# Filler products on TensorE ahead of the norms' sums and other waits, in a two-block transformer kernel

## The chip, the cores and the metric

The kernel runs on one core of a Trainium2 chip. The metric is the device time of one execution in microseconds (us); lower is better. The engines of the core work side by side, each on its own queue of instructions: TensorE (PE in the profile) multiplies matrices, VectorE (DVE) and ScalarE (ACT) work on elements, GpSimd (POOL) too, and SyncE (SP) issues transfers. A queue is worked off in the order in which its instructions stand.

## The reference, cut to what matters

Two blocks, each of two layers, on 512 tokens `x` of 1024 features. The first block has a second stream of 256 context tokens beside `x`; its mixer joins a Fourier transform, an mLSTM recurrence with gates, and a latent attention. The second block has grouped attention and dilated attention. Every layer ends in an MLP with a squared ReLU. What matters here are the norms: each is a sum over the features of every token, and its result scales everything that follows.

```python
def rmsnorm(x, g):
    y = x * rsqrt(mean(x * x, axis=-1) + EPS)
    return y * g
def modulate(h, shift, scale):
    return h * (1 + scale) + shift
...
h  = modulate(rmsnorm(x, g_norm1[l]), sh1, sc1)         # x: 512 tokens
hc = modulate(rmsnorm(xc, g_norm1[l]), sh1c, sc1c)      # context: 256 tokens
pf, mq, mk, mv, mo, mg, cq, ckv, kr = split_proj(h @ w_in[l])
kv = rmsnorm(ckv, g_kvn) @ w_ukv                        # latent keys and values
q  = rmsnorm(cq, g_qn) @ w_uq                           # latent queries
m_t = maximum(inter, dmat.max(axis=-1))                 # mLSTM: running maximum of the gates
...
x = x + ga1 * (concat([y_f, y_m, y_a]) @ w_out[l])
x = x + ga2 * (square(relu(modulate(rmsnorm(x, g_norm2[l]), sh2, sc2) @ w_up[l])) @ w_down[l])
...
return rmsnorm(x, g_final)                              # end of the first block
```

## The kernel before, in words

Features lie on the partitions, so that `x` is eight tiles of [128, 512] and the context eight of [128, 256]. Each product in full accuracy is made of three: an operand is split in a high and a low part, and `mm3` (L136) issues high·high (L143), high·low (L144) and low·high (L146, or L150 after all the others where the product has 256 columns). Weights are streamed in units: a transfer (L127), a cast of the high part on ScalarE (L120), the subtraction for the low part on GpSimd (L121). Two units have a place at a time.

A norm over the features (`norm_r`, L327) sums the squares of the eight blocks on VectorE into `acc` (L325), and lets TensorE multiply the result by a matrix of ones (L333), which adds the 128 partitions up. This sum is a product in plain float32. ScalarE and VectorE make the reciprocal root of it, and then `mod_block` scales, shifts and splits the eight blocks into `h` (L373, L374), which the next products read. The small norms of the latent keys and queries (`rms_small`, L535) do the same with one or two blocks (square L543, sum L548).

`gate_rows` (L856) prepares the gates of the mLSTM: two small products spread the gates over 64 rows (L872, L873), VectorE scans them for a running maximum `m` and a running sum (L883, L884) and subtracts (L888) into `iR`; TensorE then transposes `iR` in six pieces (L891) and spreads `m` over 128 partitions with `emsel`, once per direction (L902).

MLPs and projections whose input is a norm begin with a head (`head`, L401): the first three units of weights are run over the first half of the tokens and then over the second half (`skewed`, L389), so that the second half of the norm has time to be made. The two loops of `mlp` (L447) then run over the other units.

The framework's scheduler places every instruction on its engine's queue from the order in which the builder makes them, with its own estimates; generators in the builder weave independent work between the steps. PSUM, where TensorE writes its sums, is given out by tags (`pm`, `pt`, `p2`), with two places each.

In `build` (L1343) the start of the program runs the first modulation's products round by round (`next(first)`), then the context stream with the norm of `x` ahead, then the two layers of the first block, and then the second block.

Of the kernel before, what the change touches and what calls it, by code (L numbers as in the profile page):

```python
# [26 lines left out]
class Cols:  # L27
    """Per-feature vectors, side by side as columns of one array."""
# [33 lines left out]
def cut(t, H, classes):  # L62
    """The tokens H of t, whose order may be that of the classes modulo 4."""
    return by_classes(t)[:, :, H.start // 4:H.stop // 4] if classes else t[:, H]


def weave(a, b, na, nb):
    """Steps of two generators, in turn: nb of b spread over na of a."""
    credit = 0.0
    for _ in a:  # L70
        credit += nb / na
        while credit >= 1:
            credit -= 1
            if next(b, None) is None:
                credit = -1e9
        yield True
    for _ in b:
        yield True


class Stream:
    """Tokens whose features lie on the partitions: x, eight blocks of [128, n]."""
# [6 lines left out]
class Kernel:  # L89
# [20 lines left out]
    def psum(self, tag, shape):  # L110
        return self.ps.tile(shape, F32, tag=tag, name=tag, bufs=2)

# [10 lines left out]
    def weights(self, src, nk, nm=128, dve=False, extra=None):  # L123
        """A unit of the weights, in two parts; extra: the tag of a third place."""
# [11 lines left out]
    def mm3(self, out, w, xs, ks=None, wide=False):  # L136
        """out += w[:, i].T @ xs[i], each operand in two parts."""
# [3 lines left out]
        for i, (xh, xl) in enumerate(xs):  # L141
            k = ks[i] if ks else i
# [4 lines left out]
        if not wide:  # L147
            # short products leave the low part of the weights more time
# [3 lines left out]
    def rsqrt(self, out, mean_ps, scale, tmp, eps=EPS):  # L152
        """out = (scale * mean + eps) ** -0.5; the tables' result takes a Newton step to float32's accuracy."""
# [9 lines left out]
    def sigmoid(self, out, x, t=None):  # L163
        """out = 1 / (1 + exp(-x)), with no exponential of a positive number; with t, x is read at once."""
# [49 lines left out]
    def mod_cols(self, mod, ps, bias, at, nb, nv):  # L214
        """Rows 32 q + v of the sums to columns: mod[:, v, at + nb q + b]."""
# [3 lines left out]
        pt = self.psum("pt", [128, nb, 128])  # L219
        for b in range(nb):  # L220
# [7 lines left out]
    def gemv_now(self, r, src, out, tag, start, stop):  # L228
        """Round r of the first modulation, for both vectors, in steps, with TensorE's four column groups."""
# [17 lines left out]
    def gemvs_now(self, mod, rounds, src, bias):  # L247
        """Up to four rounds, in one tile of sums."""
# [7 lines left out]
    def gemv_later(self, mod, r, src, bias, vs):  # L256
        """A round of a modulation, in steps, on VectorE."""
# [31 lines left out]
    def until(self, n):  # L289
        """The first n of the modulations' later rounds are done."""  # L290
# [9 lines left out]
    def norm_tag(self, s, H):  # L300
        """Where the tiles of a norm lie: by halves, some are held for long, and have a place of their own."""
# [4 lines left out]
    def norm_add(self, s, k, w=None, H=None):  # L306
        """Takes block k of s.x into the sum of squares, weighted with a column of w; H: of some tokens."""
# [19 lines left out]
    def norm_r(self, s, weighted=False, H=None):  # L327
# [3 lines left out]
        ps = self.psum("pt", [128, n])  # L331
        sums = s.wsums if weighted else s.sums
# [8 lines left out]
    def scaled(self, out, x, a, r, classes):  # L341
        """out = a r x; classes: the tokens of out lie in classes modulo 4."""
# [14 lines left out]
    def norm_mod(self, s, a, sh, r=None, classes=False):  # L357
        """The normed and modulated blocks of s.x, each in two parts."""
        r = self.norm_r(s) if r is None else r
# [19 lines left out]
    def norm_steps(self, s, a, sh, weighted=False, classes=False):  # L379
        """norm_mod by halves of the tokens; the first half's norm_r is done."""  # L380
# [8 lines left out]
    def skewed(self, ws, xs, classes=False):  # L389
        """Some units over the first half of the tokens, then over the second."""  # L390
        for j, H in enumerate(HALVES):
            part = [(cut(h, H, classes), cut(l, H, classes)) for h, l in xs]
            for i, w in enumerate(ws):
# [3 lines left out]
                ps = two[:, t % 2, 0:256] if t in (2, 3) else self.psum("pt" if t == 5 else "pm", [128, 256])  # L397
                self.mm3(ps, w, part, wide=WIDE)
                yield i, H, ps

    def head(self, src, xs, extra, classes=False):  # L401
        """The first units of the products that begin in a norm."""
        return self.skewed([self.weights(src[i], 8, extra=None if i else extra) for i in range(SKEWED)], xs, classes)

    def tail(self, s, src, xs, ga, norm, hook, extra):
        """The last units of the products that end in s.x; hook: when the first half is complete."""
# [20 lines left out]
    def flush(self):  # L427
        """What waits for another unit of products: TensorE's short steps after other engines' work."""
# [7 lines left out]
    def residual(self, s, m, ps, ga, H=slice(None), classes=False):  # L436
        nc, x = self.nc, s.x[m][:, H]
        if classes:
            # from here on the tokens lie in classes modulo 4
# [7 lines left out]
    def mlp(self, ss, up, down, gas, norm=None, aside=None, head=False, hook=None, classes=False):  # L447
        """The streams' MLPs, with each unit of the weights loaded once but for the last units of two streams.
        head: the first two units by halves; hook: the last two as well; classes: s.x takes the order of s.h."""
        norm = norm or self.norm_add  # L450
        lead = 0 if len(ss) == 1 else LEAD
        for c in range(4):
            hid = [[] for _ in ss]
            for i in range(8):
# [7 lines left out]
                if c == 0 and i < lead:  # L462
                    # the first stream's first units: the second's may come later
# [38 lines left out]
    def relu2(self, s, ps, out):  # L502
        """The square of the positive part, in two parts."""
# [11 lines left out]
    # ==== first block ====  # L515
# [19 lines left out]
    def rms_small(self, s, ps_list, gains, scale, split_tag):  # L535
        """Norm over the features of up to two PSUM blocks; the result in two parts."""
# [9 lines left out]
        pm = self.psum("pt", [128, n])  # L546
        for i, sq in enumerate(sqs):
# [12 lines left out]
    def latents(self, s, l, full, ctx, o):  # L560
        """The latent attention's latents, its shared keys, and the recurrence's gates. ctx: the context's keys
        and gates, for the latent stream."""
# [1111 lines left out]
```

## Time and profile before

| | |
|---|---|
| median of 3 timed runs | 3580.7 us (3576.43 to 3587.28) |
| profiled execution, span from first to last instruction | 3586.3 us |
| TensorE busy | 3376.2 us (94%) |
| VectorE busy | 2140.4 us (60%) |
| ScalarE busy | 1456.4 us (41%) |
| GpSimd busy | 1147.3 us (32%) |
| mean granted TensorE clock | 0.971 |

The profile gives the profiled execution's time as its span, 3586.3 us; it lies between the median and the slowest of the timed runs. Busy times are read against the span. The clock is the share of TensorE's full clock that the chip granted, as a mean over the span or over a window. In the lists of instructions below, the name at the left of an arrow is the tile that is written, that at its right the tile that is read; the number in brackets is how long the engine was idle just before, with the instruction that ended this wait. Ends of products are modelled, so that the time of one is read best from the starts of neighbours.

### The profile page before, as it was taken

What the parts mean: (1) busy time and instruction counts of PE and PEld (TensorE: products, weight loads), DVE (VectorE), ACT (ScalarE), POOL (GpSimd) and SP (SyncE); (2) the same over time, 40 slices, a digit from 0 to 9 for tenths busy, and PEclk for the clock granted to TensorE, in tenths of its full rate; (3) what the DMA queues carried; (4) which work ended last, traced back from release to release, by engine and by line L of the source; (5) the groups of instructions that cost most, each with busy time, mean ns of one, the idle gap of its engine ahead of it and who ended that gap; (6) DMA issues with size and microseconds to landing.
All of it is one profiled execution on the core that took longest, in us unless ns stands there. A gap on an engine that the chain in (4) does not pass through costs nothing.

```text
span 3586.3 us, 47387 instructions
## 1 busy us (share of the span) xinstructions
PE 3376.2 (94%) x18518; PEld 2646.2 (74%) x18518; DVE 2140.4 (60%) x3006; ACT 1456.4 (41%) x2551; POOL 1147.3 (32%) x539
## 2 busy tenths in 40 slices
PE   6989998999997889989998899999999899999999
PEld 4666667888886666678777656888888757788887
DVE  5764357564457863385667977466645867454333
ACT  4545444121233554343223555543223455643222
POOL 1222033222324321144443312344444312343443
PEclk8999999999999989999999999999999999999999
DMA  7731122343335422034453101224542101222232
GB/s 268 258 117 59 32 75 89 106 130 106 106 112 179 142 68 63 21 110 144 164 173 128 65 31 52 81 91 150 170 138 94 59 30 53 75 96 88 95 100 94
DMA packets 146706, 377.88 MB, mean 105 GB/s; under 512 B 16737, under 2 KB 32690, under 8 KB 146354
## 3 DMA queue, kind: packets, MB, share of 16 engines
q1 hardware_dynamic: 146482, 374.85, 31.9%
q8 instruction: 146, 2.39, 0.3%
q14 instruction: 78, 0.64, 0.1%
HBM read 363.48 MB, written 9.86 MB: 104 GB/s over the span
## 4 chain that ended last, share of the span: by engine, by line
PE 51%; DVE 10%; issue 2%; ACT 2%; DMA 0%; POOL 0%; DVEq 0%; ACTq 0%; POOLq 0%
PE pm L143 13%; PE pm L144 13%; PE pm L146 12%; PE p L968 1%; DVE y L346 1%; PE pt L1184 1%; PE p L1166 1%; PE pt L143 1%; PE pt L144 1%; PE pm L938 1%; PE pt L1192 1%; DVE hraw L1141 1%; PE pt L1232 1%; DVE hv L159 1%; PE pm L150 1%
## 5 line engine op out<-in xcount | busy, mean ns | idle before, releaser
L121 POOL TENSOR_TENSOR wlo<-raw,whi 128x1024 fp32r<-128x1024 f32 (+2 forms) x461 | 1096.7, 2380 | 2260.7 <-ACT whi L120 2118.7
L120 ACT CAST whi<-raw 128x1024 fp32r<-128x1024 f32 (+2 forms) x468 | 477.0, 1019 | 1208.5 <-PE pm L144 987.5
L143 PE MATMUL pm<-h,whi 128*128 128x512 f32 (+1 forms) x2312 | 856.0, 379 | 9.8 <-ACT raw_s L541 3.9
L144 PE MATMUL pm<-h,whi 128*128 128x512 f32 (+1 forms) x2312 | 844.7, 373 | 0.7 <-DVE h L374 0.7
L146 PE MATMUL pm<-h,wlo 128*128 128x512 f32 x1816 | 722.4, 398 | 3.3 <-POOL wlo L121 3.3
L143 PEld LDWEIGHTS pm<-h,whi 128*128 128x128 f32 x2312 | 443.3, 192 | 104.7 <-issue 19.0
L144 PEld LDWEIGHTS pm<-h,whi 128*128 128x128 f32 x2312 | 441.9, 191 | 77.0 <-issue 5.7
L143 PE MATMUL pm<-hid,whi 128*128 128x512 f32 (+1 forms) x1280 | 462.2, 370 | 21.8 <-DVE x L445 17.5
L144 PE MATMUL pm<-hid,whi 128*128 128x512 f32 (+1 forms) x1280 | 459.9, 368 | 3.9 <-DVE hid L513 3.9
L269 DVE SCALAR_TENSOR_TENSOR ga<-g,svec,ga 128x512 f32<-128x512 f32 x280 | 337.2, 1211 | 151.5 <-DMA g<-in_w_mod 149.9
L146 PEld LDWEIGHTS pm<-h,wlo 128*128 128x128 f32 x1816 | 346.8, 191 | 80.1 <-POOL wlo L121 5.8
L146 PE MATMUL pm<-hid,wlo 128*128 128x512 f32 x976 | 384.6, 394 | 1.7 <-POOL wlo L121 1.7
L509 DVE TENSOR_TENSOR relu<-relu 128x512 f32<-128x512 f32 (+1 forms) x169 | 255.6, 1513 | 190.1 <-ACT relu L507 189.9
L445 DVE SCALAR_TENSOR_TENSOR x<-pm,mod,x 128x512 f32<-128x512 f32 (+1 forms) x184 | 125.3, 684 | 357.9 <-PE pm L146 349.4
L143 PEld LDWEIGHTS pm<-hid,whi 128*128 128x128 f32 x1280 | 244.2, 191 | 65.7 <-issue 19.6
L144 PEld LDWEIGHTS pm<-hid,whi 128*128 128x128 f32 x1280 | 243.9, 191 | 45.4 <-DVE hid L513 6.9
L146 PEld LDWEIGHTS pm<-hid,wlo 128*128 128x128 f32 x976 | 185.6, 190 | 41.5 <-POOL wlo L121 3.0
L507 ACT ACTIVATE relu<-pm 128x512 f32<-128x512 f32 (+1 forms) x160 | 85.5, 534 | 144.9 <-PE pm L146 135.7
L513 DVE TENSOR_TENSOR hid<-relu,hid 128x512 fp32r<-128x512 f32 (+1 forms) x169 | 110.1, 651 | 14.5 <-ACT hid L512 0.4
L951 ACT ACTIVATE D<-pt,cc 128x256 f32<-128x256 f32 (+1 forms) x176 | 75.0, 448 | 99.5 <-PE pt L945 59.2
L325 DVE TENSOR_TENSOR acc<-acc,sq 128x256 f32<-128x256 f32 (+1 forms) x96 | 86.7, 903 | 25.2 <-ACT sq L317 22.7
L373 ACT ACTIVATE h<-y,mod 128x256 fp32r<-128x256 f32 (+1 forms) x136 | 67.7, 528 | 81.9 <-DVE y L346 81.6
(398 smaller groups left out, 4898.6 us busy)
## 6 DMA issues: line engine op xcount, KB each, us to landing
g<-in_w_mod SPq DMA_DIRECT2D x352, 256.0 KB, 3.0
raw<-in_w_in SPq DMA_DIRECT2D x142, 512.0 KB, 3.5
raw<-in_w_down SPq DMA_DIRECT2D x136, 512.0 KB, 3.5
raw<-in_w_up SPq DMA_DIRECT2D x128, 512.0 KB, 3.5
raw<-in_w_out SPq DMA_DIRECT2D x24, 512.0 KB, 3.5
g<-in_w_mod SPq DMA_DIRECT2D x16, 512.0 KB, 7.5
raw<-in_w_out SPq DMA_DIRECT2D x16, 384.0 KB, 3.3
raw<-in_w_br SPq DMA_DIRECT2D x16, 384.0 KB, 3.0
```

What stands on the lines that cost most here:

```text
L120: nc.scalar.copy(out=hi, in_=src)
L121: (eng or nc.vector).tensor_tensor(out=lo, in0=src, in1=hi.bitcast(F32), op=ALU.subtract)
L143: nc.tensor.matmul(out, hi[:, k], xh, start=i == 0, stop=False)
L144: nc.tensor.matmul(out, hi[:, k], xl, start=False, stop=False)
L146: nc.tensor.matmul(out, lo[:, k], xh, start=False, stop=i == n - 1)
L269: nc.vector.scalar_tensor_tensor(out=a, in0=g, scalar=sk, in1=a, op0=ALU.mult, op1=ALU.add)
L325: nc.vector.tensor_tensor(out=acc, in0=acc, in1=sq, op=ALU.add)
L445: nc.vector.scalar_tensor_tensor(out=x, in0=ps, scalar=ga[:, m:m + 1], in1=x, op0=ALU.mult, op1=ALU.add)
L507: nc.scalar.activation(out=r, in_=ps, func=AF.Relu)
L509: nc.vector.tensor_tensor(out=q, in0=r, in1=r, op=ALU.mult)
L513: nc.vector.tensor_tensor(out=lo, in0=q, in1=hi.bitcast(F32), op=ALU.subtract)
L951: nc.scalar.activation(out=D[:, kk, T], in_=rp[:, kk, T], func=AF.Exp, bias=cc[:, 2 * p + kk, r:r + 1])
```

## The change

A new helper `warm` issues `n` float32 products of the matrix of ones with up to 384 columns of a table of constants (`cols`), each into the same place in PSUM as the product that follows in the builder; that product overwrites what they left. It is called ahead of the sums of `norm_r` (where `norm_mod` calls it: 2 products for 512 tokens, 4 for 256; 4 for the first half's norm after the output projection; 3 in `finish`), of `rms_small` (2 or 4), of the query products in `first_projections` (3), of the transposes in `gate_rows` (4), of the first product of a head's second half (4), and in the last three rounds of the start (2 each). `mod_cols` gets the argument too, and is called with none. The rest of the diff takes comments and docstrings out, which moves the line numbers: L143 is L149 after it, L333 is L341, L548 is L559, L891 is L904, L902 is L915.

```diff
+    def warm(self, ps, n):
+        m = min(ps.shape[-1], 384)
+        for _ in range(n):
+            self.nc.tensor.matmul(ps[:, 0:m], self.ones, self.cols[:, 0:m], start=True, stop=True)
...
-    def norm_r(self, s, weighted=False, H=None):
+    def norm_r(self, s, weighted=False, H=None, warm=0):
...
         ps = self.psum("pt", [128, n])
+        self.warm(ps, warm)
...
-        r = self.norm_r(s) if r is None else r
+        r = self.norm_r(s, warm=WARM * 384 // s.n) if r is None else r
...
-    def skewed(self, ws, xs, classes=False):
+    def skewed(self, ws, xs, classes=False, warm=0):
...
                 ps = two[:, t % 2, 0:256] if t in (2, 3) else self.psum("pt" if t == 5 else "pm", [128, 256])
+                if warm and t == len(ws):
+                    self.warm(ps, warm)
                 self.mm3(ps, w, part, wide=WIDE)
...
-        return self.skewed([...], xs, classes)
+        return self.skewed([...], xs, classes, 4)
...
         pm = self.psum("pt", [128, n])
+        self.warm(pm, WARM * 384 // n)
         for i, sq in enumerate(sqs):
             nc.tensor.matmul(pm, self.ones, sq, start=i == 0, stop=i == len(sqs) - 1)
...
             qA = [self.new("hq", [96, n], "qA") for _ in range(4)]
+            self.warm(self.psum("pt", [128, 384]), 3)
             for i in range(2):
...
         pc = self.psum("pt", [128, nblk, 64])
+        self.warm(pc.rearrange("p b e -> p (b e)"), 4)
         for b in range(nblk):
             nc.tensor.transpose(pc[:, b], iR[:, 128 * b:128 * b + 128], self.ident[0:64, 0:64])
...
+                    if i > 12:
+                        K.warm(K.psum("p2", [128, 384]), 2)
                     next(first)
...
-                            K.norm_r(X, H=H)
+                            K.norm_r(X, H=H, warm=4)
...
-                            r = K.norm_r(X)
+                            r = K.norm_r(X, warm=3)
...
+WARM = 3
```

The scheduler reacts to the new products, so that some instructions change places too. On TensorE's queue the first place is the gate rows of `x` in the first layer. `lat` is the latent queries and keys, `h` the normed input of the next unit; the six transposes read `iR`, the `emsel` products read `m`. Before:

```order
L146 MATMUL pm<-lat,wlo 128x512
L143 MATMUL pm<-lat,whi 128x512
L144 MATMUL pm<-lat,whi 128x512
L146 MATMUL pm<-lat,wlo 128x512
L891 MATMUL pt<-ident,iR 128x64 x6
L902 MATMUL pt<-m,emsel 128x512
L143 MATMUL pm<-h,whi 128x512
L902 MATMUL pt<-m,emsel 128x512
L144 MATMUL pm<-h,whi 128x512
L146 MATMUL pm<-h,wlo 128x512
```

And after, where the `L628` and the `lat` rows are products that stood ahead of the first row above:

```order
L915 MATMUL pt<-m,emsel 128x512
L628 MATMUL pm<-wlo,lat 128x384
L149 MATMUL pm<-lat,whi 128x512
L150 MATMUL pm<-lat,whi 128x512
L152 MATMUL pm<-lat,wlo 128x512
L904 MATMUL pt<-ident,iR 128x64 x6
L149 MATMUL pm<-lat,whi 128x512
L150 MATMUL pm<-lat,whi 128x512
L152 MATMUL pm<-lat,wlo 128x512
L149 MATMUL pm<-lat,whi 128x512
L150 MATMUL pm<-lat,whi 128x512
L915 MATMUL pt<-m,emsel 128x512
```

The transposes and both `emsel` products stand ahead of some 15 products on `lat` that came before them, three fillers follow the second `emsel` product, and four more stand some 18 rows further up, ahead of the first products on `lat`.

The second place is the context's keys of the second layer, in the MLP of the first; `sq_s` is the square that the small norm sums, `hid` the MLP's hidden values. Before:

```order
L150 MATMUL pm<-h,wlo 128x256 x8
L143 MATMUL pm<-hid,whi 128x512
L144 MATMUL pm<-hid,whi 128x512
L146 MATMUL pm<-hid,wlo 128x512
L143 MATMUL pm<-hid,whi 128x512
L144 MATMUL pm<-hid,whi 128x512
L548 MATMUL pt<-sq_s,ones 128x256
L146 MATMUL pm<-hid,wlo 128x512
```

And after:

```order
L156 MATMUL pm<-h,wlo 128x256 x8
L117 MATMUL pt<-cols,ones 128x256 x4
L559 MATMUL pt<-sq_s,ones 128x256
L149 MATMUL pm<-hid,whi 128x512
L150 MATMUL pm<-hid,whi 128x512
L152 MATMUL pm<-hid,wlo 128x512
L149 MATMUL pm<-hid,whi 128x512
```

Four fillers take the place behind the last product of `h`, and the sum has moved ahead of five products of the MLP.

The third place is the head of the last MLP, where the last product over the first half (`wlo`) is followed by the first unit over the second half, which reads a weight kept from the first half. Before:

```order
L143 MATMUL pm<-h,whi 128x256
L144 MATMUL pm<-h,whi 128x256
L150 MATMUL pm<-h,wlo 128x256
L143 MATMUL p_27008<-h,w_26930 128x256
L144 MATMUL p_27008<-h,w_26930 128x256
```

And after:

```order
L150 MATMUL pm<-h,whi 128x256
L156 MATMUL pm<-h,wlo 128x256
L117 MATMUL p_27100<-cols,ones 128x256 x4
L149 MATMUL p_27100<-h,w_27022 128x256
L150 MATMUL p_27100<-h,w_27022 128x256
```

Four fillers stand between the two halves; nothing else moved there.

## Rows read from the trace of the kernel before

**Rows 1.** The page's part 1: busy us, share of span, instructions, by engine.

```profile
PE 3376.2 (94%) x18518; PEld 2646.2 (74%) x18518; DVE 2140.4 (60%) x3006; ACT 1456.4 (41%) x2551; POOL 1147.3 (32%) x539
```

**Rows 2.** The cores: span in us, mean granted TensorE clock.

```profile
core 0: 3586.3 us, clock 0.971
```

**Rows 3.** TensorE's waits: engine, tile, line, releaser: us, times, longest.

```profile
PE pt L333 <- DVE acc L325: 12.7, 5, 3.8
...
PE pt L548 <- DVE sq_s L543: 9.7, 7, 3.5
...
PE pt L891 <- DVE iR L888: 4.2, 1, 4.2
```

**Rows 4.** TensorE in time: start us, us, instruction [idle before <-releaser].

```profile
5.80 1.08 PE L243 MATMUL pt<-g,cst 128*32 128x256 f32 x8 [5.80 <-DMA g<-in_w_mod]
...
85.06 0.62 PE L243 MATMUL p<-g,cst 128*32 128x256 f32 x4 [1.58 <-DMA g<-in_w_mod]
...
237.62 0.80 PE L143 MATMUL pm<-h,whi 128*128 128x512 f32 x1 [3.91 <-ACT raw_s L541]
...
278.59 0.90 PE L891 MATMUL pt<-ident,iR 64*128 64x64 f32 x6 [4.18 <-DVE iR L888]
...
577.83 0.70 PE L333 MATMUL pt<-acc,ones 128*128 128x256 f32 x2 [2.82 <-DVE acc L325]
...
699.38 0.47 PE L143 MATMUL pm<-hid,whi 128*128 128x512 f32 x1 [1.62 <-DVE x L445]
...
1143.59 1.22 PE L548 MATMUL pt<-sq_s,ones 128*128 128x256 f32 x2 [3.47 <-DVE sq_s L543]
...
2049.14 1.38 PE L333 MATMUL pt<-acc,ones 128*128 128x512 f32 x2 [3.06 <-DVE acc L325]
```

**Rows 5.** Windows: us, busy us (instructions) by engine, PEclk, DMA share, GB/s.

```profile
236.00:240.00 4.00, 2.15 (x5) 1.24 (x5) 2.75 (x5) 2.83 (x4) 2.30 (x2) 0.67 0.43 127
...
240.00:244.00 4.00, 4.00 (x8) 2.48 (x9) 1.80 (x3) 1.93 (x3) 0.00 (x0) 0.50 0.27 65
...
278.00:288.00 10.00, 9.41 (x21) 5.10 (x22) 4.75 (x8) 1.81 (x3) 1.77 (x1) 0.52 0.29 80
...
578.00:582.00 4.00, 4.00 (x12) 3.13 (x13) 2.72 (x7) 1.39 (x4) 0.00 (x0) 0.59 0.40 135
...
700.00:704.00 4.00, 4.00 (x19) 3.29 (x18) 3.08 (x4) 0.00 (x0) 0.81 (x1) 1.00 0.29 75
...
1140.00:1148.00 8.00, 4.53 (x11) 3.48 (x11) 5.97 (x9) 0.89 (x2) 1.86 (x1) 0.62 0.60 197
...
1258.00:1272.00 14.00, 13.54 (x30) 7.95 (x31) 7.84 (x10) 4.33 (x7) 4.03 (x2) 0.51 0.31 103
...
1960.00:1966.00 6.00, 6.00 (x52) 6.00 (x51) 2.94 (x8) 1.98 (x7) 0.00 (x0) 1.00 0.29 95
...
2048.00:2054.00 6.00, 4.86 (x12) 3.37 (x13) 6.00 (x11) 2.69 (x7) 0.00 (x0) 0.72 0.02 9
...
2780.00:2784.00 4.00, 4.00 (x21) 4.00 (x21) 3.96 (x5) 2.25 (x4) 2.40 (x1) 0.53 0.00 0
```

**Rows 6.** TensorE in time around a float32 sum of 512 columns.

```profile
252.73 0.39 PE L146 MATMUL pm<-h,wlo 128*128 128x512 f32 x1
252.95 1.02 PE L548 MATMUL pt<-sq_s,ones 128*128 128x512 f32 x2
...
254.04 0.39 PE L144 MATMUL pm<-h,whi 128*128 128x512 f32 x1
```

**Rows 7.** TensorE in time around a float32 sum of 256 columns.

```profile
2762.50 0.67 PE L333 MATMUL pt<-acc,ones 128*128 128x256 f32 x2
...
2763.12 0.28 PE L143 MATMUL p<-hid,whi 128*128 128x256 f32 x1
2763.24 0.28 PE L144 MATMUL p<-hid,whi 128*128 128x256 f32 x1
```

**Rows 8.** VectorE in time: the scan that writes m.

```profile
272.98 1.25 DVE L883 TENSOR_TENSOR_SCAN m<-p,m,iR 32x512 f32<-32x512 f32 x1
```

More of the change, by code (lines that the diff above doesn't have):

```diff
@@ L212, in new_mod, with mod_cols @@
         return self.const.tile([128, nv, 48], F32, name=name)
-    def mod_cols(self, mod, ps, bias, at, nb, nv):
+    def mod_cols(self, mod, ps, bias, at, nb, nv, warm=0):
         nc = self.nc
@@ L219, in mod_cols @@
         pt = self.psum("pt", [128, nb, 128])
+        self.warm(pt.rearrange("p b e -> p (b e)"), warm)
         for b in range(nb):
@@ L401, in head @@
     def head(self, src, xs, extra, classes=False):
-        return self.skewed([self.weights(src[i], 8, extra=None if i else extra) for i in range(SKEWED)], xs, classes)
+        return self.skewed([self.weights(src[i], 8, extra=None if i else extra) for i in range(SKEWED)], xs, classes, 4)
     def tail(self, s, src, xs, ga, norm, hook, extra):
```

## The prediction

> **What bounds the kernel now.** I read four views in this order: the page's busy times, the span with its mean clock, TensorE's waits, and then single waits and windows in time. TensorE is busy 94% of the span [rows 1], so the kernel ends when TensorE's queue is empty; a product added to that queue costs its own length unless it falls into a wait. Over the span of 3586.3 us TensorE idles 210 us (3586.3 − 3376.2). Its mean granted clock was 0.971 [rows 2]. As the clock has two levels, 2.4 and 1.2 GHz, 0.971 means 2 × 0.029 × 3586 = 208 us at the lower one, and holding the clock up everywhere could give back at most half of that, 104 us. That is the prize the fillers can compete for, and the waits are the room they have for nothing: the norms' sums (L333, L548) waited 12.7 and 9.7 us in all, the transposes of the gate rows (L891) 4.2 us [rows 3].
>
> What a wait does to the clock stands in two pairs of rows. At 237.62 a product starts after 3.91 us of waiting for ScalarE's copy `raw_s` in the key norm of X, and 240 to 244 is at 0.50; before 577.83 the queue waited 2.82 us, and in 578 to 582 the clock is 0.59. A product at 699.38 had waited 1.62 us, and 700 to 704 stayed at 1.00 [rows 4, 5]. So in this trace a piece of 1.6 us did no harm, one of 2.8 us did.
>
> **The price of a filler.** All are float32 products, like the norms' own sums. Between the start of L548 at 252.95 and of L144 at 254.04 lie this sum and one ordinary product, 1.09 us; an ordinary product takes 0.22 us (252.73 to 252.95), so 512 columns cost 0.86 us at the full clock [rows 6]. For 256 columns, 2762.50 to 2763.12 is 0.62 us with one ordinary product of 0.12 in it (2763.12 to 2763.24): 0.50 us, against 0.43 by halving the 512 [rows 7]. I take 0.65 us for 384 columns, 0.43 to 0.50 for 256, 0.22 for 128, and double at the low clock. In the changed queue there are 90 fillers: 38 of 384, 48 of 256 and 4 of 128 columns. All exposed, they cost 38 × 0.65 + 48 × 0.43 + 4 × 0.22 = 46 us (50 with 0.50); all hidden, nothing.
>
> **The change part by part.** On the other engines nothing is added; some instructions change places.
> 1. Heads of the products (fillers before the second half's first unit, five heads, 4 × 256 each). At those five places TensorE has no wait: 1960 to 1966 is busy 6.00 of 6.00 at 1.00. The head at 2780 to 2784 is busy 4.00 of 4.00 too, at 0.53 [rows 5]. The fillers stand behind the last product of the first half, not in a wait. 20 × 0.43 = 8.6, two of them at half clock: +9.
> 2. Key norm of X, first layer: 4 × 0.65 = 2.6 us fall into the 3.91 us before 237.62 [rows 4]; a piece of 1.3 us is left, less than the 1.62 that did no harm. The low stretch behind it (240 to 244 at 0.50) goes: 236 to 240 at 0.67 and 240 to 244 at 0.50 hold 2.6 + 4 us of low clock [rows 5], half of which is 3.3: −3.
> 3. Gate rows of X, both layers. Four fillers stand before the block of `lat` products and three behind the second L902. Also the first L902, the transposes and the second L902 are now ahead of some 15 products on `lat` which TensorE had finished by 274.41, before it waited 4.18 us for iR until 278.59 [rows 4]. The scan of VectorE that writes m ends at 272.98 + 1.25 = 274.23 [rows 8]. In the new order TensorE reaches L902 at 271 to 272, waits until 274.2, does four products, waits until 278.6, and then has some 15 products left (15 × 0.22 = 3.4) plus 3 fillers (1.95), less one L902 done early (1.0): +4.4 if the clock is as before. Half of 278 to 288 was lost to the clock (0.52 [rows 5], up to 5 us), and that is −5 if the smaller pieces keep it up. I take +2.5 for each layer, +5 in all; bounds −1 and +12 together.
> 4. Context key norm of layer two: 4 × 0.43 = 1.7 us in the wait of 3.47 before 1143.59 [rows 4], hidden. But L548 has moved ahead of five products (5 × 0.22 = 1.1) that used to run before it, and they now come behind: +1.2. The idle piece left is 3.47 + 1.1 − 1.7 = 2.9, again of the harmful size, so no clock is counted back in 1140 to 1148 (0.62 [rows 5]).
> 5. Context norm: four fillers, then one product, then L333, which is moved ahead of eight of X's products. It waited until 577.83 for VectorE's sum [rows 4], and the eight (8 × 0.22 = 1.8) now run behind it; the wait becomes 2.82 + 1.8 = 4.7 in one piece: +2.5 with the clock.
> 6. Finish of the first block (3 × 0.65): L333 is moved ahead of nine products (2.1 us); it waited 3.06 us until 2049.14 [rows 4]. The fillers hide, the nine do not, and the order of the attention after it is stirred: +3, bounds −2 and +7. (2048 to 2054 is at 0.72 [rows 5]; half of that could come back.)
> 7. Start and context stream (to 80 us): the first five fillers lie in the wait of 5.80 us for the first weights [rows 4], at nothing. Of those between 35 and 78 us (0.8 in a wait, 4 × 0.43 + 4 × 0.22 + 5 × 0.65 = 5.9 exposed) about half is lost again in the later waits for weights, such as 1.58 us at 85.06 [rows 4]: +3, bounds 0 and +7.
> 8. The rest (the norm of layer two's X, the context norm in the MLP, halves of the output projection): fillers that stand behind products without a wait, 0.8 + 2 + 1 + 0.5: +4.
> 9. The moved order itself shifts when TensorE idles elsewhere; I count back 4 us of clock for the low stretches near items 4, 6 and 8, a third of the 12 that they could give (1140 to 1148 at 0.62 is 3 us of lost half, 2048 to 2054 at 0.72 about 1.7, and others like them): −4, bounds −12 and 0.
>
> Sum: 9 − 3 + 5 + 1.2 + 2.5 + 3 + 3 + 4 − 4 = +20.7. The profiled execution's span of 3586.3 us is 5.6 above the median of 3580.7, and inside the timed runs (3576.43 to 3587.28). So +20 stands on the median: 3600.
>
> Of items 3 to 6 the rows show that nothing runs behind a waiting product: TensorE does nothing between 274.41 and 278.59, with the products on `h` queued behind the transposes [rows 4]. The Trainium skill, "TensorE: Matmul & The Clock Gate", Part 2, step ① of "Step-by-step: what each phase is for", says the same in general: only weight loads are pulled ahead, "The MATMULs themselves stay in program order". By this rule the moved products cost about 8 us; if TensorE could pass a waiting product they would cost nothing, and the sum would be 3592. The trace agrees with the rule.
>
> **The rivals.** (a) The fillers hold the clock. If a few microseconds of filler work keep TensorE's clock up behind every wait that they stand in, not only behind the key norm, low stretches go at the key norm (3.3), the gate rows of both layers (278 to 288 at 0.52: 4.8; 1258 to 1272 at 0.51: 6.9), the context keys (3.0), the context norm (1.6) and the finish (1.7): 21 us back [rows 5]. Items 3 to 6 fall to nothing, and 16 us of fillers without a wait (items 1, 7, 8) remain: 3581 − 21 + 16 = 3576. These stretches hold 43 of the 208 us; if a quarter of the other 165 goes as well, 20 us more come back: 3556. I take the middle, 3566. For it speaks 699.38; against it that most fillers stand where TensorE did not wait, and that the moved sums lengthen the same waits. The point that decides is the granted clock in 278 to 288. Beside it stands the Trainium skill, the same page, "HAM oscillation — how this bites in real kernels": idle pieces throttle the clock and the penalty is half of the throttled time; by it a well placed filler pays, and 208 us throttled is 104 us of penalty, as my ceiling. The trace agrees in kind.
> (b) Absorbed. The fillers lie in waits or shorten later ones: behind a head, VectorE and the weights may be the ones that are late, so that 9 us vanish, and items 7 and 8 too. 0.971 would stay and the time would be about 3585. Against it: those stretches are busy 6.00 of 6.00 [rows 5].
> (c) Nothing is hidden: all 90 are exposed (+46) and the moved products cost 8 more, with 4 of clock lost: about 3639. Against it: the waits of rows 4 are real.
>
> **How the numbers follow.** Forecast (items as summed, 3592 to 3612): 0.50. (a) 0.17; (b) 0.22; (c) 0.11. The kernel's runs differ by 0.3% between lowest and highest, so within 0.3% (3570 to 3591) counts as no change. (a) gives faster mostly below 3570: 0.16 of its chance with a little of (b); (b), half of the forecast's low edge and the rest of (a) make 0.25 no change; the forecast and (c) make 0.59 slower. The range 3568 to 3624 leaves out a part of (a) and most of (c), together less than 2 in 10; the forecast's own range is 3592 to 3612.
>
> **What would show it.** Right: TensorE's busy time about 45 us above 3376.2, its idle time about 25 us below 210, the low time near 200 us and the five heads longer by 1.7 us each; after the key norm the stretch at 0.50 is gone. Wrong: a mean clock above 0.980 (rival a), heads no longer than before (b), or idle time as before (c). My largest single doubt is item 3: whether 278 to 288 is at 0.5 or 1.0.

## The result, and the profile after

The changed kernel took 3619.9 us (median of 4 runs, 3618.2 to 3623.9), the one before 3581.8 beside it: a ratio of 1.010 with an interval of 1.008 to 1.012, that is 38 us more by the medians, some 36 by the ratio. The time lies in the stated range of 3568 to 3624 and on the forecast side, but at nearly twice the forecast step of 20 us: it is above the 3592 to 3612 that the items were to give, and about as near to rival (c), 3639, as to the forecast, 3600. The spans of the two profiled executions differ by 31.0 us. First the page's busy times of the kernel after, then its span and clock:

```profile
PE 3421.7 (95%) x18698; PEld 2679.1 (74%) x18698; DVE 2144.3 (59%) x3006; ACT 1459.2 (40%) x2551; POOL 1147.1 (32%) x539
```

```profile
core 0: 3617.3 us, clock 0.973
```

TensorE's busy time rose by 45.5 us [rows 1], as forecast; its idle time fell from 210 to 196 us (3617.3 − 3421.7), by 14 and not by 25. The low time, which is the time at the lower clock, fell from 208 to 195 us (2 × 0.027 × 3617; [rows 2]). The mean clock is printed to three places, so that each such figure is good to some 4 us; summed from the clock records of the two traces it is 205 and 199. TensorE's waits by line (engine, tile, line, releaser: us, times, longest; L341 was L333, L559 was L548):

```profile
PE pt L341 <- DVE acc L332: 11.5, 5, 4.2
...
PE pt L559 <- DVE sq_s L553: 10.0, 6, 3.3
...
PE pt L705 <- ACT vt L700: 9.7, 3, 5.5
...
PE pt L117 <- DVE V L707: 1.1, 1, 1.1
```

The norms' sums wait about as long as before [rows 3], though fillers stand ahead of them, the six transposes L904 are no longer in the list, and two waits are longer or new: transposes of L705, which wait for a copy (6.1 us before, as L693), and a filler (L117) that itself waits for its place in PSUM, which VectorE reads till then (`V`). TensorE in time (start us, us, instruction, idle before and releaser), at the key norm, at a head and at the finish:

```profile
233.87 2.74 PE L117 MATMUL pt<-cols,ones 128*128 128x384 f32 x8
...
237.96 0.50 PE L149 MATMUL pm<-h,whi 128*128 128x512 f32 x1 [1.35 <-ACT raw_s L551]
...
240.27 1.72 PE L559 MATMUL pt<-sq_s,ones 128*128 128x512 f32 x2 [1.11 <-DVE sq_s L553]
...
1600.19 1.89 PE L117 MATMUL p<-cols,ones 128*128 128x256 f32 x8
...
1601.73 0.47 PE L149 MATMUL p<-h,w 128*128 128x256 f32 x1
...
2066.50 1.82 PE L341 MATMUL pt<-acc,ones 128*128 128x512 f32 x2 [3.76 <-DVE acc L332]
```

Eight records are four fillers. At the key norm they fill the old wait [rows 4]; 1.35 us of it is left, but the sum behind it still starts at 240.27, when VectorE has made the square, as it did at 239.92 before. At the head, where nothing waits, 1600.19 to 1601.73 is spent on fillers. The gate rows of the two layers; the last two lines are from the kernel before:

```profile
277.10 0.58 PE L904 MATMUL pt<-ident,iR 64*128 64x64 f32 x6
...
280.73 1.23 PE L915 MATMUL pt<-m,emsel 64*128 64x512 f32 x2 [1.69 <-DVE cc L906]
...
1258.47 0.69 PE L626 MATMUL pm<-whi,lat 128*128 128x384 f32 x1 [2.80 <-ACT kA L619]
```

```profile
1258.46 0.80 PE L143 MATMUL pm<-lat,whi 128*128 128x512 f32 x1 [3.61 <-ACT qA L645]
...
1260.90 0.90 PE L891 MATMUL pt<-ident,iR 64*128 64x64 f32 x6
```

In the first layer the transposes L904 do not wait for `iR` any more, and the second `emsel` product waits 1.69 us instead. In the second layer the transposes did not wait for `iR` before either: TensorE waited 3.61 us for `qA`, ahead of them, and now it waits 2.80 us for `kA`. Windows at the places of [rows 5] (busy us of each engine, then the granted clock):

```profile
240.00:244.00 4.00, 3.73 (x8) 2.36 (x9) 2.12 (x4) 2.00 (x4) 0.00 (x0) 0.58 0.24 62
...
278.00:288.00 10.00, 8.31 (x24) 4.71 (x23) 3.34 (x4) 4.13 (x8) 1.27 (x1) 0.83 0.17 52
...
582.00:586.00 4.00, 4.00 (x12) 3.15 (x11) 3.40 (x9) 1.95 (x5) 0.00 (x0) 0.57 0.33 119
...
1260.00:1274.00 14.00, 13.79 (x34) 7.97 (x35) 6.82 (x8) 5.88 (x11) 2.36 (x1) 0.59 0.26 84
...
2100.00:2120.00 20.00, 13.72 (x49) 7.46 (x47) 13.77 (x25) 8.04 (x17) 2.35 (x1) 0.66 0.08 27
```

The low time behind the key norm became 3.3 us instead of 6.6; 278 to 288 is at 0.83 instead of 0.52; the second layer's gate rows are hardly better (0.59 for 0.51); and 2100 to 2120 has 13.6 us of low time (2 × 0.34 × 20), with 13.72 of 20 us busy, where the kernel before had 6.8 (2080 to 2100, at 0.83).

Where the 31 us came in can be read from the starts of the same products in both traces. The table gives how much each stretch (times of before) grew, for the kernels that matter below; the heads are their five steps together.

| stretch | after | heads alone | twice | none | no finish | four waits |
|---|---|---|---|---|---|---|
| 0 to 228 | 0.3 | 1.7 | 3.1 | 1.4 | 1.5 | 0.8 |
| key norm, gate rows 1 (to 300) | 2.9 | −0.3 | 0.9 | 0.7 | 2.9 | −1.7 |
| to 620 | 2.2 | −0.1 | 2.1 | 4.5 | 3.2 | 0.2 |
| MLP 1 (to 1010) | −0.5 | 0.3 | 0.0 | 4.2 | −1.2 | 3.9 |
| context keys (to 1200) | −2.7 | −0.3 | −1.4 | −4.4 | −2.2 | −6.9 |
| gate rows 2 (to 1400) | 7.9 | 0.0 | 1.8 | 5.4 | 4.7 | −0.1 |
| to 1575 | 3.4 | 2.4 | 2.6 | 2.5 | 2.6 | 0.0 |
| five heads | 10.8 | 9.6 | 17.0 | 1.1 | 9.3 | 0.9 |
| finish, attention (2010 to 2300) | 6.5 | −0.7 | 3.4 | 6.9 | −0.3 | −2.8 |
| all else | 0.1 | −0.7 | 1.0 | 1.3 | 1.4 | 0.3 |
| sum | 31.0 | 11.8 | 30.4 | 23.7 | 21.8 | −5.4 |

Single stretches move by 1 to 4 us where nothing was changed (the 2.4 up to 1575 stands in "heads alone", and about as much or more in every other trace but those of the kernel before and of the four waits), so only larger or repeated steps are read. Two steps repeat. Gate rows 2 grew by 4.7 to 7.9 us in the six traces with the changed order in which the fillers stand once or not at all or late, by 1.1 and 1.8 in the two with twice the fillers in place, and by 0.2 at most in the five that have the old order there. And the finish, read from 2030 on, since some traces are shifted by 3 us at 2010 and no longer at 2030, grew by 3.4 to 7.0 us in the eight traces with fillers or their order there, and not at all in the five without (−2.2 to 0.0).

### The profile page after: what moved, and what is told of

Its sections match the earlier page's. It is cut to its first block, busy times and chain, and to the rows that moved or that the text cites. A ratio compares the mean times of both kernels' runs of the same rounds, so it can differ in the third digit from the quotient of the medians.

```text
span 3617.3 us, 47751 instructions
## 1 busy us (share of the span) xinstructions
PE 3421.7 (95%) x18698; PEld 2679.1 (74%) x18698; DVE 2144.3 (59%) x3006; ACT 1459.2 (40%) x2551; POOL 1147.1 (32%) x539
## 4 chain that ended last, share of the span: by engine, by line
PE 68%; DVE 15%; issue 4%; DMA 3%; ACT 2%; POOL 0%; DVEq 0%; SPq 0%; ACTq 0%; POOLq 0%
PE pm L149 17%; PE pm L150 17%; PE pm L152 15%; DMA g<-in_w_mod 3%; PE p L981 3%; DVE ga L276 2%; PE pm L156 2%; DVE y L354 2%; PE pm L951 1%; PE pt L1197 1%; DVE acc L332 1%; PE p L830 1%; PE p L1179 1%; PE pt L958 1%; PE pt L848 1%
## 5 line engine op out<-in xcount | busy, mean ns | idle before, releaser
L149 PE MATMUL pm<-h,whi 128*128 128x512 f32 (+1 forms) x2312 | 854.0, 378 | 1.4 <-ACT raw_s L551 1.3
L149 PEld LDWEIGHTS pm<-h,whi 128*128 128x128 f32 x2312 | 441.1, 191 | 91.6 <-issue 13.9
L149 PE MATMUL pm<-hid,whi 128*128 128x512 f32 (+1 forms) x1280 | 463.6, 371 | 18.9 <-DVE x L455 15.7
L149 PEld LDWEIGHTS pm<-hid,whi 128*128 128x128 f32 x1280 | 245.5, 192 | 62.5 <-issue 17.9
```

Of the source, the lines that this page charges most:

```text
L149: nc.tensor.matmul(out, hi[:, k], xh, start=i == 0, stop=False)
```

## The experiments

Theories: **length** (a filler outside a wait costs its own time, the moved order costs nothing), **order** (the moved products cost 10 us or more), **clock** (the fillers pay a part of their time back through TensorE's clock). The order of the queues depends on the fillers' size as the scheduler sees it; therefore fillers were edited in the finished queues, after scheduling, where the order had to stay. Every group of runs has its own runs of the kernel before beside it (medians of 3581.8 to 3586.3 us); between groups the ratios are compared, and 0.001 of ratio is 3.6 us.

**All fillers cut to 16 columns, order kept.**

```diff
+    def cut(a):
+        return a.__replace__(ap=[list(v) for v in a.ap[:-1]] + [[a.ap[-1][0], 16]])
...
+            if i.name in FILL:      # after scheduling
+                blk.instructions[k] = i.__replace__(ins=[cut(i.ins[0]), i.ins[1]], outs=[cut(i.outs[0])])
```

> The changed kernel with every instruction in its place, but each filler cut to 16 columns after the queues were set, so that 90 fillers cost about 90 x 0.03 = 3 us instead of 45. Theory L (length: a filler outside a wait costs its own length, the changed order costs nothing): about 3585, and the heads' steps of 1.7 to 2.7 us go. Theory O (order: products that were moved behind a waiting one come late): at least 3595, the steps at the gate rows, the finish and the sums stay. Theory C (clock: the fillers earn a part of their length back by holding TensorE's clock up): the low time rises from 195 towards 208 us or above, and the time falls by clearly less than 42 us from 3620.

3613.8 us, ratio 1.0075 (1.0058 to 1.0092): 6 us less than with full fillers, 9 by the ratios, and not 35. One reason is that a short filler is not free. A head of this kernel:

```profile
1605.22 0.96 PE L117 MATMUL p<-cols,ones 128*128 128x16 f32 x8
...
1606.03 0.36 PE L149 MATMUL p<-h,w 128*128 128x256 f32 x1
```

Four fillers of 16 columns last 0.81 us (1605.22 to 1606.03) less an ordinary gap, about 0.2 us each, against 0.4 with 256 columns. So 90 of them cost some 20 us (an estimate, 90 × 0.2), not 3: my expectation was wrong there. The other reason is the clock:

```profile
core 0: 3612.0 us, clock 0.969
```

0.969 is 224 us of low time, 29 more than with full fillers (23 by the clock records), which is worth 12 to 14 us. Length alone falls.

**The heads' fillers alone, on the old order, and the change without them.**

```diff
-        self.warm(pm, WARM * 384 // n)      # first kernel: here and at all other places but the heads
+        pass
...
-        return self.skewed([...], xs, classes, 4)     # second kernel: only this
+        return self.skewed([...], xs, classes, 0)
```

> The kernel before with the heads' fillers alone (20 of 256 columns); nothing else in TensorE's queue moves. Theory L: five steps of 1.7 to 2.0 us, +9 us, 3591. Theory O: nothing moved, so 3582. Theory C: the low stretches around the heads (1946 to 1958, 2772 to 2784) get shorter and the sum is below +9.

> The changed kernel without the heads' fillers, all else in the same order on TensorE. Theory L: 9 to 10 us less than 3620, that is 3610. Theory O: 3620, as the order stays. Theory C: above 3610, since the clock behind the heads falls.

3599.0 (1.0041; 1.0027 to 1.0055) and 3605.8 (1.0071; 1.0054 to 1.0088). In the traces the five steps are 9.6 us with the fillers alone, as theory length expected, and 0.7 instead of 10.8 us without. The first kernel's time is 15 us above the kernel before, and not 9; of the rest, 2.4 us came up to 1575 and 1.7 in the start, where nothing was edited. At the heads, where TensorE has no wait, length holds.

**Every filler twice, order kept.**

```diff
+            if i.name in FILL:      # after scheduling
+                blk.instructions.insert(k + 1, i.__replace__(name=f"I-{9000000 + len(blk.instructions)}", sync_info=None))
```

> The changed kernel with every instruction in its place and each filler issued twice (180 fillers). Theory L: what lies outside a wait doubles and the waits are used up: +45 at most, about 3655 to 3665. Theory O: little more than 3620. Theory C: low time clearly under 195 us and a time under 3640.

3622.8 us, 1.0112 (1.0092 to 1.0131), within the error of the change itself: 90 more fillers, of some 45 us, cost 4 us or so, which the errors do not tell from nothing. The busy times, the clock, and the windows of both gate rows:

```profile
PE 3440.6 (95%) x18878; PEld 2697.2 (75%) x18878; DVE 2141.7 (59%) x3006; ACT 1458.1 (40%) x2551; POOL 1149.3 (32%) x539
```

```profile
core 0: 3616.6 us, clock 0.982
```

```profile
278.00:288.00 10.00, 10.00 (x38) 6.15 (x38) 3.23 (x4) 4.40 (x9) 2.64 (x1) 1.00 0.17 52
...
1260.00:1280.00 20.00, 16.74 (x63) 10.48 (x64) 12.07 (x14) 10.08 (x17) 4.23 (x3) 1.00 0.20 60
```

The busy time rose by 18.9 us only, the idle time fell by 20 to 176 us, and the low time fell to 130 us (0.982), by 65 to 69 us. Both gate rows run at the full clock, and the second's step is 1.8 instead of 7.9 us. The heads paid their 17.0 us in full. So away from the heads the clock theory holds: the second set of fillers paid for itself, no more.

**The order nearly alone.** All fillers without semaphores taken out after scheduling, the others cut to 16 columns (28 stayed, fewer than I had counted).

```diff
+                if s is None or not (len(s.on_wait) or len(s.on_update)):
+                    del blk.instructions[k]
+                    continue
+                blk.instructions[k] = i.__replace__(ins=[cut(i.ins[0]), i.ins[1]], outs=[cut(i.outs[0])])
```

> The changed kernel with every other instruction in its place, and 53 of the 90 fillers taken out of TensorE's queue after the order was set (those that carry no semaphore); the other fillers, which have to stay for the order, are cut to 16 columns (0.25 us each in the run with all fillers cut). This leaves the changed order nearly alone. Theory A (account: time = the kernel before + the fillers' own time - the idle time that they fill - half of the low time that they lift; the order itself costs nothing): some 9 us of fillers, idle time near 205 to 212 us, low time near 220 us, 3590 to 3598. Theory O (the moved order costs 10 us or more): idle time above 220 us and 3605 or more.

3609.3 us, 1.0066 (1.0047 to 1.0084): 24 us above the kernel before with hardly a filler left. Clock, busy time and the two sums' waits:

```profile
core 0: 3610.0 us, clock 0.969
```

```profile
PE 3391.0 (94%) x18574; PEld 2661.1 (74%) x18574; DVE 2144.1 (59%) x3006; ACT 1458.3 (40%) x2551; POOL 1148.7 (32%) x539
```

```profile
PE pt L341 <- DVE acc L332: 18.6, 6, 6.5
...
PE pt L559 <- DVE sq_s L553: 13.2, 7, 4.9
```

The sums wait 18.6 and 13.2 us instead of 12.7 and 9.7 [rows 3], 9.4 us more; the idle time is 219 us, and the low time 224. The time is what the order theory expected (3605 or more); the idle time is just short of the 220 us that it named. About 28 × 0.2 = 6 us of the 24, at most, are the length of the fillers that stayed; they also keep their waits, so the order does not stand quite alone.

**Twice, without the heads', in place and directly ahead of the sums.**

```diff
+            if type(i).__name__ == "InstMatmult" and held.get(place(i)):   # second kernel alone
+                new += held.pop(place(i))     # fillers without semaphores, held back till here
+            new.append(i)
```

> The kernel with every filler issued twice, less the heads' fillers, which showed no return in the clock. Theory A: the run with all fillers twice less the 17 us of its heads' steps: 3600 to 3604, low time about 130 us. A theory that the heads' fillers too hold the clock up: low time nearer 160 us and a time above 3610.

> As the run with every filler twice and none in the heads, but the fillers that carry no semaphore stand directly ahead of the product that will overwrite them (the norm's sum or the transposes) and not where the scheduler put them; 22 fillers that have no such product are left out. Theory A: the same fillers fill more idle time when they stand in the wait itself, idle time falls below 170 us, 3585 to 3592. Rival: place is all one for the clock and the time, 3595 to 3602. Rival 2: fillers directly ahead of a sum delay it, and what follows waits: above 3605.

3602.7 (1.0048; 1.0029 to 1.0068) as the account (theory A) foresaw, and 3616.7 (1.0083; 1.0062 to 1.0105), as rival 2 did; the second kernel has 22 fillers less. The steps fit rival 2 (key norm and gate rows 1: 5.1 us instead of 1.0; gate rows 2: 5.1 instead of 1.1): on the changed order many a sum does not wait, so that fillers right ahead of it delay the sum and what needs it. That this is the cause was not tried by itself. Of the other 12 us between the two profiles, 6 came between 1600 and 1940, where no filler stands; they stay unexplained.

**The finish.** The change without the three fillers of `finish`, and these three alone on the kernel before.

```diff
-    r = K.norm_r(X, warm=3)
+    r = K.norm_r(X)                 # first kernel; the second has only this warm=3
```

> The changed kernel without the three fillers of the first block's last norm (finish); TensorE's order in the attention after it goes back to that of the kernel before, the rest stays as changed. Theory O (the moved order costs, most at this place): the steps between 2020 and 2180 us, +6 to +7 in every run with the changed order and -2 in the runs with the old one, turn to -2: 3610 to 3613, and the low stretch of 13.6 us near 2100 shrinks to 6.8. Theory A (the order costs nothing): the three fillers hide in a wait, so 3618 to 3620.

> The kernel before with the three fillers of finish alone; on TensorE 41 instructions change places, all in the second block's first attention. Theory O: +8 to +9 between 2020 and 2180 us, 3590 to 3592. Theory A: no change, 3581 to 3584.

3609.5 (1.006; 1.0045 to 1.0076) and 3597.5 (1.0033; 1.0018 to 1.0048). Taking out three fillers of 0.65 us saves 10 us by the medians and 14 by the ratios; alone they cost about 12 (6 to 17), where 8 to 9 was expected. From 2030 to 2300 the two traces show −0.3 instead of 6.5, and 6.5 where the other traces with the old order there give −2.2 to 0.0. With twice the fillers it is 3.4, with hardly one 7.0: it is the order that costs, and the fillers give some of it back. TensorE's waits from 2030 to 2140 with the three alone:

```profile
PE pt L341 <- DVE acc L332: 3.7, 1, 3.7
...
PE pt L705 <- ACT vt L700: 3.7, 1, 3.7
...
PE pt L117 <- DVE V L707: 1.0, 1, 1.0
```

The filler waits for its own place in PSUM; the sum, moved ahead of nine products, waits 3.7 us (3.06 before, [rows 4]); and transposes that did not wait before wait 3.7 us. The low time near 2100 was 13.5 to 17.0 us in each of the eight traces with this order, 6.8 in that of the kernel before, 6.7 in the change without these fillers, and no more than that in the other traces without them. The kernel before there:

```profile
2080.00:2100.00 20.00, 17.54 (x78) 9.19 (x79) 17.55 (x33) 11.84 (x28) 2.36 (x1) 0.83 0.08 28
```

**Fillers in the waits, nothing moved.** On the kernel before, fillers set into the finished queue directly ahead of eight waiting products, then of four of these, then of three, whose waits are filled about half. The four were chosen because they had gained in the trace with eight.

```diff
+PLAN = {("N",4):(4,256), ("N",11):(4,384), ("N",8):(3,256), ("N",6):(1,384),   # L333, by its n-th
+        ("R",4):(6,256), ("R",5):(3,384), ("T",1):(5,384), ("M",18):(14,128)}  # L548, L891, L221
...
+PLAN = {("T",1):(5,384), ("M",18):(14,128), ("R",4):(6,256), ("N",6):(1,384)}  # four
...
+PLAN = {("T",1):(3,384), ("M",18):(7,128), ("R",4):(3,256)}                    # half
```

> The kernel before with nothing moved and 40 fillers set into its finished queue, directly ahead of eight products that waited 1.4 to 4.7 us in its trace (transposes of the gate rows at 278.6, sums at 577.8, 1143.6, 1189.1, 1225.2, 1568.4 and 2049.1, transposes at 1125.8), each group about 0.3 to 1 us shorter than the wait. Theory A: the fillers cost nothing, idle time falls by some 18 us, and of the 208 us of low time the stretches behind these waits go (278 to 290, 578, 1124 to 1132, 1142 to 1150, 1186 to 1194, 2050: up to 40 us, half of it time): 3562 to 3575. Rival: so short a piece of work does not move the clock: 3580 to 3584. Rival 2: the sums come late: 3588 or more.

> The kernel before with nothing moved and fillers at four of the eight waits alone: the gate rows' transposes at 278.6 (5 of 384 columns), the transposes at 1125.8 (14 of 128), the sums at 1143.6 (6 of 256) and 1189.1 (1 of 384). Theory W (fillers that stand in a long wait keep the clock up and cost nothing): -5.4, -4.4, -2.4 and -1.5 us as in the profile with eight, 3568 to 3573. Rival G (what they give is taken back later, in waits for VectorE in the MLP and in other low stretches): 3580 to 3584.

> As the run with four waits, but each wait filled about half (3 of 384 columns at the gate rows, 7 of 128 and 3 of 256; none at 1189.1), so that idle pieces of 2 to 3 us stay. If idle pieces over about 1.6 us let the clock fall, as the kernel before shows, the low stretches behind these waits stay and the time is that of before, 3581 to 3584. If any work in the wait is enough, as with the full waits: under 3575, or the stretches at 278 and 1124 to 1150 are gone.

Eight: 3586.4 us, 1.0008 (0.9992 to 1.0023), no change, where 3562 to 3575 was forecast. Its profiled execution, the slowest of the twelve, lost 19.0 us in the first MLP, where nothing was edited: TensorE's idle time there grew by 10.6 us and its busy time by 8.5, at a clock of 0.96 instead of 0.99. Elsewhere it had gained 3.4. Of the idle time 8.2 us are one wait, for VectorE's residuals `x`, in that stretch, 620 to 1010:

```profile
PE pm L143 <- DVE x L445: 19.8, 5, 4.0
```

This wait came to between 8.6 and 19.8 us in the 14 traces (11.6 in that of the kernel before), with the same queue order too. That it makes the runs of one kernel spread, 3574 to 3599 for the kernel before, is likely and was not tested. Four: 3578.7 us, 0.9977 (0.9965 to 0.9989), **faster than both kernels**, by 8 us of 3586, where 3568 to 3573 was forecast. Half: 3581.9, 0.9981 (0.9969 to 0.9992), not to be told from the four. The four's filled waits at the gate rows and at 1125.8, and the windows behind:

```profile
274.76 3.39 PE L333 MATMUL pt<-cols,ones 128*128 128x384 f32 x10
...
279.10 0.58 PE L891 MATMUL pt<-ident,iR 64*128 64x64 f32 x6 [0.95 <-DVE iR L888]
...
1123.92 3.29 PE L333 MATMUL pt<-cols,ones 128*128 128x128 f32 x28
...
1128.79 0.33 PE L221 MATMUL pt<-ident,gsb 128*128 128x128 f32 x1 [1.58 <-ACT gsb L218]
```

```profile
278.00:288.00 10.00, 9.05 (x24) 5.28 (x24) 5.28 (x8) 1.81 (x3) 2.00 (x2) 0.66 0.29 80
...
1130.00:1146.00 16.00, 14.97 (x79) 12.43 (x78) 11.21 (x9) 5.37 (x9) 7.55 (x3) 1.00 0.61 206
```

Of the wait of 4.18 us [rows 4] 0.95 is left, of that at 1125.8 (4.69 before) 1.58. 1130 to 1146 is at 1.00; in the kernel before 1140 to 1148 was at 0.62 [rows 5]. The context keys gained 6.9 us, forecast were 8.3 with the sum at 1189.1; the gate rows gained 1.7 and not 5.4, and 278 to 288 is at 0.66, 6.8 us of low time, where the trace with eight had none. In the half-filled kernel these waits were

```profile
287.66 0.58 PE L891 MATMUL pt<-ident,iR 64*128 64x64 f32 x6 [2.25 <-DVE iR L888]
...
1126.87 0.33 PE L221 MATMUL pt<-ident,gsb 128*128 128x128 f32 x1 [3.14 <-ACT gsb L218]
```

and yet the low time behind 1126.9 was 3.4 us, where the kernel before had 6.8, and 6.8 behind 287.7, where it had 9.6 (2 × 0.48 × 10, [rows 5]). That idle pieces of 2 to 3 us bring the whole low stretch back, as was expected, did not hold in this trace; as low stretches also come and go, one trace does not settle it.

## Why the prediction was right, and where it was not

The sign, the busy time (+45.5) and the stated range were right; the size was forecast at half to two thirds of what came (20 against 31 by the profile, 36 by the runs), and the items' own range, 3592 to 3612, was missed. Two terms were too small by more than the noise, the gate rows and the finish; the others err by less than 3 us, both ways, and partly cancel, which is luck.

- Item 1, heads: right. +9 forecast, 9.6 measured on the old order and 10.8 in the change. Rival (b), absorbed, falls.
- Item 2, key norm: −3 forecast, about −0.4 measured. The step that failed is that the low stretch was on the path: half of it went, but the sum waits for VectorE's square until 240 in both kernels.
- Item 3, gate rows: +5 forecast, 10.8 measured (2.9 + 7.9), within the bounds of −1 to 12, but the path was read wrongly in both layers. In the first, the forecast has TensorE wait for `iR` until 278.6, as before; the transposes did not wait at all (277.10), and the second `emsel` product did, for 1.69 us. In the second layer item 3 takes the same path, but the kernel before has a single wait for `iR` [rows 3], in the first; what TensorE waited for there was `qA`. And the clock's share, where I took the middle between as before and kept up, did not come: 0.59 stayed. With hardly a filler left this stretch still grew by 5.4 us, with twice the fillers by 1.8: the order costs, and enough fillers bring most of it back through the clock.
- Items 4 and 5: +1.2 and +2.5 forecast; 0.3 at the context keys' sum, and 1.1 at the context norm, both within what stretches move by themselves.
- Item 6, finish: +3 forecast, 6.5 measured in the trace and 10 to 14 by the runs, above my bound of 7. It comes from the moved order: 7.0 from 2030 on with the fillers all but gone, −0.3 with the old order. I counted nine products behind the sum, and not the transposes behind these, nor that a filler itself has to wait for its place in PSUM.
- Items 7 and 8: 0.3 for 3, and 3.4 (up to 1575) for 4, of which some 2.4 stand in traces too where nothing was changed there.
- Item 9, clock: −4 forecast; 208 to 195 us of low time is −6.5, and −3 by the clock records (205 to 199).

The premise beneath items 1, 7 and 8, that a filler outside a wait costs its own time, holds only where the clock is up and no wait is near. Away from the heads twice as many cost nothing, because low time and idle time fall by as much. What the change lost there is the order: 18 to 24 us with hardly a filler left, of which I had counted 8 for the moved products. Rival (a) had the right mechanism and the wrong yield: the fillers lift the clock, and by 65 us of low time when doubled, but that was used up by the order and the heads. Rival (c), as near in time as the forecast, falls by its sign: the idle time did not stay as before, and twice the fillers cost next to nothing away from the heads. The Trainium skill, "TensorE: Matmul & The Clock Gate", "HAM oscillation — how this bites in real kernels", counts half of the throttled time as the penalty. The run with cut fillers agrees in kind: shorter by some 25 us in all (an estimate, 45 − 20), they lowered TensorE's busy time by only 14.6 us (3421.7 to 3407.1), with 23 to 29 us more of low time, half of which is 12 to 14.

The 36 us of the change are then about 10 for the heads, 10 to 14 for the finish, and the rest for the moved order at the gate rows and the sums, less what the clock gave. This split rests on runs with errors of some 5 us each. How much of the first gate rows' step is order and how much fillers at half clock (281.89 to 285.18 for three) is open: with hardly a filler it is 0.7 instead of 2.9, in one trace.

What item 3 overlooked stands in the kernel before too. The subtraction that makes `iR` took 3.10 us there beside one of GpSimd's, and 0.95 in the change, where the next one, L908, met GpSimd's and took 3.02:

```profile
275.44 3.10 DVE L888 TENSOR_TENSOR iR<-iR,cum 64x768 f32<-64x768 f32 x1
...
275.38 2.34 POOL L121 TENSOR_TENSOR wlo<-raw,whi 128x1024 fp32r<-128x1024 f32 x1 [1.95 <-ACT whi L120]
```

```profile
276.09 0.95 DVE L900 TENSOR_TENSOR iR<-iR,cum 64x768 f32<-64x768 f32 x1
277.07 3.02 DVE L908 TENSOR_TENSOR cum<-cum,m 64x768 f32<-64x768 f32 x1
```

So about 2 of the 4.18 us that TensorE waited before [rows 4] hung on when GpSimd's subtraction fell (3.10 − 0.95), and in all eight traces with the changed order at the gate rows the transposes' wait for `iR` is gone.

## What to carry to other kernels

Filler work paid here only where nothing else moved: look at the order of the queue first, and set fillers directly ahead of the product that waits, in waits that the trace shows, shorter than the wait. With the fillers in the builder the scheduler moved the awaited products and their neighbours, and that cost 18 to 24 of the 36 us; that the cause is the filler's early claim on a place in PSUM is likely and was not tried. At the heads, where TensorE is busy, a filler was pure loss. Look, too, whether the wait that is to be filled stays where it is once the order changes.

## What the hardware showed

A float32 filler of 16 columns costs 0.2 us where one of 256 costs 0.4: a sixteenth of the columns saves only half. Doubling 70 fillers away from the heads cost no time that the runs can tell, with 65 to 69 us less of low time. The VectorE subtractions that write `iR` and `cum` took 0.95 us, and 2.3 to 3.1 in each of the 12 cases, of 56 in the 14 traces, in which one of GpSimd's ran beside it for over 1.4 us. And not every low stretch follows an idle piece: in the kernel before, TensorE is busy from 258 on, in 262 to 264 mostly with the gate rows' products of 16 rows (L872, L873), and the clock is down in the next stretch:

```profile
262.00:264.00 2.00, 2.00 (x7) 0.66 (x5) 1.56 (x2) 1.58 (x4) 1.81 (x1) 1.00 0.02 4
...
264.00:268.00 4.00, 4.00 (x11) 2.54 (x11) 1.69 (x3) 3.38 (x6) 0.00 (x0) 0.59 0.73 204
```
